# Scale and shift of the first norm, moved from the ends of the MLP into its middle, with the result kept in DRAM

## The chip, the cores and the metric

The kernel runs on one core of a Trainium2 chip. The metric is device time of one execution in microseconds (us), lower is better. The profile comes from one further execution of the same program; its times are counted from the start of the span.

## The reference

Two layers process 512 latent tokens and, in the first layer only, 256 context tokens, each of width 1024. Only the end of a layer matters here:

```python
x_mid = layer_norm(ALPHA * x + gt1 * mix, ln1_g[l], ln1_b[l])
ff = squared_relu_mlp(x_mid * (1.0 + sc2) + sh2, mlp_w1[l], mlp_w2[l])
x = layer_norm(ALPHA * x_mid + gt2 * ff, ln2_g[l], ln2_b[l])
```

A layer norm subtracts a row's mean, divides by its deviation, and then multiplies by `g` and adds `b`, both vectors of 1024 channels. `x_mid` is used twice: as the MLP's input (the channel mixing) and as the residual of the second norm.

## The kernel before

Tokens are handled in tiles of 128 rows by 1024 channels: six in layer 0 (latent tiles 2 to 5, context tiles 0 and 1), four in layer 1. A layer ends in four steps: the output projection (`out_proj`, PSUM tiles `po`), the first norm tile by tile (`norm_tile` in `done`), the transposition of the normalized tiles into the MLP's input (`to_T`, PSUM tiles `pT`, results `xh` and `xl`), the MLP (`mlp`), and the second norm (`done2`). The MLP walks over eight slices `f` of the hidden channels; each does a first product (PSUM tiles `ph`) and a second one (PSUM tiles `pf`, added to `ff` on VectorE, L1814). Weights come through `raw` (L204, 512 KB loads on SyncE's queue into two buffers `wraw`) and `unit` (L215 on ScalarE and L216 on VectorE split them into a high and a low part `whi` and `wlo`). PSUM tiles of the products rotate through four banks.

The normalized tile is stored to DRAM (`xm`) without `g` and `b` of the first norm. For the MLP's input these are folded into the scale and shift of `to_T`. For the second norm's residual, `residual` loads a tile of `xm` into one of three buffers `lnx` and applies the two rows `gr2` on GpSimd (POOL), one multiplication (L1691) and one addition (L1692) over 128x1024. In the text `fetch2` calls it three times before the last slice's second product and then once after each finished tile; but a scheduler orders the instructions of each engine by a simulated timeline, and it places loads as soon as their buffers are free.

`norm_tile` is the second place that matters: L1700 adds the residual and sums the row, L1702 on ScalarE sums the squares, L1703 to L1713 are eleven VectorE instructions on one number per row (Newton steps L1711 and L1712 on `lst` and `lsi`), and L1714 on ScalarE writes the normalized tile.

Of the kernel before, what the change touches and what calls it, by code (L numbers as in the profile page):

```python
# [8 lines left out]
F32 = mybir.dt.float32  # L9
# [18 lines left out]
D = 1024  # L28
T = 768
# [105 lines left out]
class Net:  # L135
# [62 lines left out]
    def raw(self, src, stage=None):  # L198

        if stage is None:  # L200
            r = self.wp.tile([128, 1024], F32, name="wraw", bufs=2)
        else:
            r = stage.tile([128, 1024], F32, name="wraw", bufs=12)
        self.nc.sync.dma_start(r, src)  # L204
        return r

    def unit(self, src, stage=None):
# [667 lines left out]
    def qkv(self, l, hi, lo, A, ctx_out, tick, gate):  # L875
# [25 lines left out]
        def norm(raw, t0, x):  # L901

            g, cg, sg = tab[x]
            n = (6 - t0) * 4
            r = raw[:, t0:].rearrange("p t h d -> p (t h) d")
            ss = p.tile([128, 24], F32, name="nss", bufs=2)
            for t in range(t0, 6):
                w = p.tile([128, 4, 64], F32, name="nsq")
                nc.scalar.activation(w, raw[:, t], AF.Square)
                v.reduce_sum(ss[:, 4 * (t - t0):4 * (t - t0) + 4], w, axis=AX.X)  # L910
            v.tensor_scalar(ss[:, :n], ss[:, :n], 1.0 / 64, RMS_EPS, op0=ALU.mult, op1=ALU.add)
            rs = self.rsqrt(p, ss[:, :n], n, "nr", 24)
            v.tensor_mul(r, r, rs.unsqueeze(2).to_broadcast([128, n, 64]))
            if t0 == 0:
                c = raw[:, 0:2].rearrange("p t h d -> p (t h) d")
                nc.gpsimd.tensor_tensor(c, c, g.unsqueeze(1).to_broadcast([128, 8, 64]), op=ALU.mult)
            for t in range(4):
                o = p.tile([128, 4, 64], F32, name="nro")
                def hv(a):
                    return a.rearrange("p x (a h d) -> p x a h d", a=2, h=2)  # L920
                v.tensor_mul(hv(o), hv(raw[:, t + 2])[:, :, :, ::-1],
                             sg[:, t].rearrange("p (a h d) -> p a h d", a=2, h=2)
                             .unsqueeze(1).to_broadcast([128, 4, 2, 2, 16]))
                nc.gpsimd.tensor_tensor(raw[:, t + 2], raw[:, t + 2], cg[:, t].unsqueeze(1).to_broadcast([128, 4, 64]),
                                        op=ALU.mult)
                v.tensor_add(raw[:, t + 2], raw[:, t + 2], o)
# [32 lines left out]
        def keys(raw):  # L959
            norm(raw, 0, 1)  # L960
            for h in range(4):
                if h in GK:
                    gblock()
                ks = p.tile([128, 6, 2, 64], F32R, name="qs", bufs=2)
                nc.scalar.copy(ks[:, :, 0], raw[:, :, h])
                v.tensor_sub(ks[:, :, 1], raw[:, :, h], ks[:, :, 0])
                kf = ks.bitcast(F32)
                kT = p.tile([128, T], F32R, name="kT", tag="qT", bufs=2)
                T_((kf, 0), 0, (kT[:64], kT[64:]), 64)
                nc.sync.dma_start(A["k"][h].bitcast(F32), kT.bitcast(F32))  # L970
                kT = p.tile([128, T], F32R, name="kT", tag="qT", bufs=2)
                T_((kf, 0), 1, (kT[:64],), 64)
                tick(1.3)
                for x in range(2):
                    nc.sync.dma_start(A["kl"][h, 64 * x:64 * x + 64].bitcast(F32), kT[:64].bitcast(F32))
# [740 lines left out]
    def affine(self, l, ln, lm, sc, sh):  # L1716

        v = self.nc.vector
        m = self.modv[lm]
        g = self.cp.tile([128, 2, 8], F32, name=f"ag{l}{ln}")  # L1720
        b = self.cp.tile([128, 2, 8], F32, name=f"ab{l}{ln}")
        s1 = m[:, :, 8 * sc:8 * sc + 8]
        v.tensor_mul(g, s1, self.v(l, f"ln{ln}_g").unsqueeze(1).to_broadcast([128, 2, 8]))
        v.tensor_mul(b, s1, self.v(l, f"ln{ln}_b").unsqueeze(1).to_broadcast([128, 2, 8]))
        v.tensor_add(b, b, m[:, :, 8 * sh:8 * sh + 8])
        return g, b
# [43 lines left out]
            if t >= 2:  # L1770
                done(t)

    def mlp(self, l, hi, lo, ctx, tt, ff, p, pm, late, fetch, done):


        nc, v = self.nc, self.nc.vector
        spans = [(TC, TL)] + ([(0, TC)] if ctx else [])
        for f in range(8):
            hh = pm.tile([128, 4, T], F32R, name="hh", tag="q4", bufs=4)
            hl = pm.tile([128, 4, T], F32R, name="hl", tag="q4", bufs=4)  # L1780
            if f:
                parts = [(b, spans) for b in range(4)]
            else:
                parts = [(b, [s]) for s in spans for b in range(4)]
            U1 = {}
            for b, sp in parts:
                if b // 2 not in U1:
                    U1[b // 2] = self.unit(self.i["mlp_w1"][l, 0, 2 * f + b // 2])
                    if l + 1 < L and b == 0:
                        self.mod_unit(l + 1, f)  # L1790
                wh, wl = U1[b // 2]
                if f == 0 and b == 0 and sp[0][0] == 0:
                    late()
                for o, n in sp:
                    ps = self.pd.tile([128, 512], F32, name="ph", tag="pd")
                    self.mmB(ps[:, :n], wh, wl, 128 * (b % 2), hi, lo, o, n, 8, 256)
                    r = p.tile([128, 512], F32, name="hr", bufs=2)
                    nc.scalar.activation(r[:, :n], ps[:, :n], AF.Relu)
                    q = p.tile([128, 512], F32, name="hq", bufs=2)
                    v.scalar_tensor_tensor(q[:, :n], ps[:, :n], 0.0, r[:, :n], op0=ALU.max, op1=ALU.mult)  # L1800
                    nc.scalar.activation(hh[:, b, o:o + n], q[:, :n], AF.Copy)
                    v.tensor_sub(hl[:, b, o:o + n], q[:, :n], hh[:, b, o:o + n])

            if l + 1 < L and f == 7:
                self.mod_end(l + 1, 0, 16)

            def job(c, t):
                ps = self.pd.tile([128, 512], F32, name="pf", tag="pd")
                self.mmA(ps, *U[c], hh, hl, 128 * t, 4, 512)
                d = ff[t][:, 512 * c:512 * c + 512]  # L1810
                if f == 0:
                    nc.scalar.copy(d, ps)
                else:
                    v.tensor_add(d, d, ps)  # L1814
            if M1 + f - 1 == 24:
                self.mod_end(l, 2 * M1, 48)
            U = []
            if f < 7:
                for c in range(2):
                    U.append(self.unit(self.i["mlp_w2"][l, f, c]))  # L1820
                    if c == 0 and f and M1 + f - 1 < 24:
                        self.mod_unit(l, M1 + f - 1)
                    for t in tt:
                        job(c, t)
            else:
                for _ in range(3):
                    fetch()
                for c in range(2):
                    U.append(self.unit(self.i["mlp_w2"][l, f, c]))
                for t in tt:  # L1830
                    job(0, t)
                    job(1, t)
                    if t >= 2:
                        done(t)


    def forward(self):
        nc, v = self.nc, self.nc.vector
# [10 lines left out]
        hi, lo = self.split_pair(px)  # L1849
# [4 lines left out]
        for u in range(8):  # L1854
            self.mod_unit(0, u, p0, cols)
            if u >= 2:
                t = (LAT + CTX)[u - 2]
# [13 lines left out]
        for l in range(L):  # L1871
            ctx = l < L - 1
            tt = LAT + (CTX if ctx else [])
# [75 lines left out]
            pm = self.pool(f"pm_{l}", es=eh)  # L1949
# [3 lines left out]
            ph = self.pool(f"ph_{l}", es=eh)  # L1953
# [4 lines left out]
            xm = self.dp.tile([T, D], F32, name=f"xm{l}")  # L1958
# [23 lines left out]
            hi, lo = self.split_pair(px)  # L1982
# [6 lines left out]
            ff = {t: fa[:, t] for t in tt}  # L1989
            gr2 = [self.row(ph, self.i[f"ln1_{x}"][l], "ln" + x) for x in "gb"]  # L1990
            if not ctx:
                gr3 = [fa[:, 0], fa[:, 1]]
                for g, x in zip(gr3, "gb"):
                    nc.sync.dma_start(g, self.i[f"ln2_{x}"][l].partition_broadcast(128))
            res2, later2 = {}, list(tt)

            def fetch2():
                t = later2.pop(0)
                res2[t] = self.residual(ph, xm[128 * t:128 * t + 128], gr2)
            xn = self.dp.tile([T, D], F32, name=f"xn{l}")  # L2000

            def done2(t):
# [11 lines left out]
            def late():  # L2014
                self.to_T(hi, lo, ph, "hq", y6, *ag, 1)

            self.mlp(l, hi, lo, ctx, tt, ff, ph, pm, late, fetch2, done2)
            if ctx:
                hi, lo = self.split_pair(px)
                ag = self.affine(l, 2, l + 1, 1, 0)  # L2020
# [29 lines left out]
```

## Time and profile before

| | |
|---|---|
| median of 3 runs | 3540.79 us (3539.16 to 3541.75) |
| the profiled execution | 3549.5 us, its span 3547.4 us |
| TensorE (PE) busy | 3214.4 us, 91% of the span |
| VectorE (DVE) busy | 2222.9 us, 63% |
| ScalarE (ACT) busy | 1556.0 us, 44% |
| GpSimd (POOL) busy | 458.4 us, 13% |
| granted TensorE clock, mean | 0.941 |

The busy shares are means over stages with different limits. The profiled execution is 8.7 us longer than the median of the three runs; 2.1 us of its time lie outside its span.

### The profile page before, as it was taken

How to read it: one execution, taken by the hardware profiler on the slowest of the kernel's cores; microseconds unless marked ns; L12 is line 12 of the kernel's file. 1: busy time of each engine (PE TensorE's matmuls, PEld its weight loads, DVE VectorE, ACT ScalarE, POOL GpSimd, SP SyncE). 2: the span in 40 equal slices, each digit the busy share in tenths (PEclk: the TensorE clock that was granted, in tenths of full speed). 3: DMA queues.
4: the chain of work that ended last, by engine and by line, in shares of the span. 5: the costliest groups of instructions: out<-in, count | busy, mean ns of one | idle time of the engine just before them, and what ended most of it. 6: DMA issues, size and time to landing. Idle time of an engine off the chain costs nothing. (4 is left out here: it accounts for less than half of the span.)

```text
span 3547.4 us, 62497 instructions
## 1 busy us (share of the span) xinstructions
PE 3214.4 (91%) x24309; PEld 2663.3 (75%) x24309; DVE 2222.9 (63%) x4528; ACT 1556.0 (44%) x3146; POOL 458.4 (13%) x615
## 2 busy tenths in 40 slices
PE   7999999979997997999999798878969997979996
PEld 5888888857765897888888686766857775867775
DVE  2888378856878346333335697748948786563445
ACT  2444456556776213322222353436657673233222
POOL 0102022222000121000001001212224000420000
PEclk9999999978998998999999899989969998989998
DMA  5545566575542543222322445437656526533331
GB/s 185 159 136 158 170 181 193 172 194 137 147 127 74 168 144 119 81 93 90 108 72 74 133 136 161 147 104 216 194 170 152 133 70 192 178 123 119 113 107 66
DMA packets 419535, 487.32 MB, mean 137 GB/s; under 512 B 235940, under 2 KB 302500, under 8 KB 419112
## 3 DMA queue, kind: packets, MB, share of 16 engines
q1 hardware_dynamic: 408744, 458.02, 42.3%
q0 software_dynamic: 10496, 25.31, 2.7%
q8 instruction: 192, 3.15, 0.4%
q14 instruction: 103, 0.84, 0.1%
HBM read 355.27 MB, written 127.94 MB: 136 GB/s over the span
## 5 line engine op out<-in xcount | busy, mean ns | idle before, releaser
L215 ACT CAST whi<-wraw 128x1024 fp32r<-128x1024 f32 x288 | 293.4, 1048 | 555.6 <-PE pf L322 162.0
L216 DVE TENSOR_TENSOR wlo<-wraw,whi 128x1024 fp32r<-128x1024 f32 x288 | 360.1, 1272 | 243.2 <-ACT whi L215 240.1
L310 PE MATMUL ph<-xh,whi 128*128 128x512 f32 (+1 forms) x768 | 277.1, 362 | 2.4 <-DVE xTf L1744 2.4
L311 PE MATMUL ph<-xl,whi 128*128 128x512 f32 (+1 forms) x768 | 276.0, 360 | 3.0 <-DVE xl L1746 3.0
L312 PE MATMUL ph<-xh,wlo 128*128 128x512 f32 (+1 forms) x768 | 276.0, 360 | 0.0
L320 PE MATMUL pf<-whi,hh 128*128 128x512 f32 x640 | 253.4, 396 | 1.1 <-DVE ff L1814 0.6
L321 PE MATMUL pf<-wlo,hh 128*128 128x512 f32 x640 | 252.6, 395 | 0.0
L322 PE MATMUL pf<-whi,hl 128*128 128x512 f32 x640 | 251.6, 397 | 0.0
L1066 DVE TENSOR_REDUCE st<-pS 128x1 f32<-128x384 f32 x288 | 152.1, 536 | 116.3 <-PE pS L1064 113.8
L310 PE MATMUL pga<-xh,whi 128*128 128x512 f32 (+1 forms) x576 | 213.3, 370 | 1.6 <-ACT kT L950 1.6
L311 PE MATMUL pga<-xl,whi 128*128 128x512 f32 (+1 forms) x576 | 211.3, 367 | 0.0
L312 PE MATMUL pga<-xh,wlo 128*128 128x512 f32 (+1 forms) x576 | 210.5, 365 | 0.0
L1814 DVE TENSOR_TENSOR ff<-ff,pf 128x512 f32<-128x512 f32 x140 | 94.9, 686 | 177.9 <-PE pf L322 177.8
L1067 ACT ACTIVATE P<-pS,st 128x384 f32<-128x384 f32 x288 | 164.1, 572 | 77.0 <-DVE st L1066 72.3
L1691 POOL TENSOR_TENSOR lnx<-lnx,lng 128x1024 f32<-128x1024 f32 x14 | 35.8, 2565 | 1039.1 <-DMA lnx<-xm 1005.6
L310 PEld LDWEIGHTS ph<-xh,whi 128*128 128x128 f32 x768 | 146.1, 190 | 30.5 <-issue 2.9
L311 PEld LDWEIGHTS ph<-xl,whi 128*128 128x128 f32 x768 | 146.0, 190 | 27.2 <-DVE xl L1746 3.5
L310 PE MATMUL pm<-yh,whi 128*128 128x512 f32 (+1 forms) x384 | 141.5, 373 | 25.6 <-ACT whi L215 19.7
L312 PEld LDWEIGHTS ph<-xh,wlo 128*128 128x128 f32 x768 | 145.7, 190 | 23.5
L1101 DVE TENSOR_TENSOR pl<-pPT,ph 128x512 fp32r<-128x512 f32 x208 | 141.4, 684 | 32.9 <-ACT ph L1100 31.4
L320 PE MATMUL pat<-whi,xh 128*128 128x256 f32 x512 | 148.6, 290 | 2.0 <-ACT kT L950 1.8
L1063 PE MATMUL pS<-kT,qT 128*128 128x384 f32 x288 | 127.6, 444 | 23.0 <-ACT P L1067 18.1
(468 smaller groups left out, 8706.7 us busy)
## 6 DMA issues: line engine op xcount, KB each, us to landing
wraw<-in_mlp_w_dram SPq DMA_DIRECT2D x128, 512.0 KB
wraw<-in_w_in_dram SPq DMA_DIRECT2D x108, 512.0 KB
wraw<-in_mod_w_dram SPq DMA_DIRECT2D x96, 512.0 KB
SUV<-rV SPq DMA_DIRECT2D x192, 64.0 KB
BK<-rBK SPq DMA_DIRECT2D x24, 512.0 KB
rZK<-ZK SPq DMA_DIRECT2D x20, 512.0 KB
Z<-rZK SPq DMA_DIRECT2D x40, 256.0 KB
G<-gst SPq DMA_DIRECT2D x24, 384.0 KB
```

The lines of the kernel that those rows point to most:

```text
L215: nc.scalar.copy(h[:, c], r)
L216: nc.vector.tensor_sub(lo[:, c], r, h[:, c])
L310: nc.tensor.matmul(ps, h, a, start=(first and k == 0), stop=False)
L311: nc.tensor.matmul(ps, h, b, start=False, stop=False)
L312: nc.tensor.matmul(ps, lw, a, start=False, stop=(last and k == kt - 1))
L320: nc.tensor.matmul(ps, a, h, start=(k == 0), stop=False)
L321: nc.tensor.matmul(ps, a, lw, start=False, stop=False)
L322: nc.tensor.matmul(ps, b, h, start=False, stop=(k == kt - 1))
L1063: nc.tensor.matmul(ps[:, :w], qT[h][:, o:o + 128], kT[:, ks], start=True, stop=False)
L1066: v.reduce_max(nm, ps[:, :w], axis=AX.X, negate=True)
L1067: nc.scalar.activation(P[:, ks], ps[:, :w], AF.Exp, bias=nm, accum_out=sm)
L1101: v.tensor_sub(pl, pt, ph)
```

## The change

`residual` with `gr2` is called inside the MLP, once after each weight unit of the second product from the second slice on (`affine`): it loads a tile of `xm`, multiplies and adds on GpSimd, and GpSimd's own queue stores the result to a new DRAM tensor `xr`. The second norm's residual is then loaded from `xr`, with nothing to apply. Both kinds of load are ordered behind the last weight load that was issued before them (`issue_after`), so that the scheduler can't place them earlier.

```diff
         else:
             r = stage.tile([128, 1024], F32, name="wraw", bufs=12)
-        self.nc.sync.dma_start(r, src)
+        self.w_dma = self.nc.sync.dma_start(r, src)
         return r
...
                     if c == 0 and f and M1 + f - 1 < 24:
                         self.mod_unit(l, M1 + f - 1)
+                    if f:
+                        affine()
                     for t in tt:
                         job(c, t)
...
-            res2, later2 = {}, list(tt)
+            xr = self.dp.tile([T, D], F32, name=f"xr{l}")
+            res2, later2, plain = {}, list(tt), list(tt)
+
+            def affine():
+
+                if plain:
+                    t = plain.pop(0)
+                    rows = slice(128 * t, 128 * t + 128)
+                    with self.tc.issue_after(self.w_dma.ins):
+                        x = self.residual(ph, xm[rows], gr2)
+                    nc.gpsimd.dma_start(xr[rows], x)
 
             def fetch2():
                 t = later2.pop(0)
-                res2[t] = self.residual(ph, xm[128 * t:128 * t + 128], gr2)
+                with self.tc.issue_after(self.w_dma.ins):
+                    res2[t] = self.residual(ph, xr[128 * t:128 * t + 128], None)
```

TensorE's order of instructions is the same in both programs. On SyncE's queue, between the output projection and the MLP of layer 0, three loads of `xm` stand between the stores of the normalized tiles before:

```order
L1689 DMA lnx<-in_x_dram 128x1024
L1689 DMA lnx<-xm_15002 128x1024
L1977 DMA xm_15002<-y_14998 128x1024 x2
L1689 DMA lnx<-xm_15002 128x1024
L204 DMA wraw<-in_mod_w_dram 128x1024 x2
L1689 DMA lnx<-xm_15002 128x1024
L1977 DMA xm_15002<-y_14998 128x1024 x2
L204 DMA wraw<-in_mlp_w_dram 128x1024 x2
L260 DMA modp_93<-modo 2x256 x4
```

Now none is there; the first two stand in the MLP's second slice, one behind each unit:

```order
L1689 DMA lnx<-in_x_dram 128x1024
L1979 DMA xm_15002<-y_14998 128x1024 x2
L204 DMA wraw<-in_mod_w_dram 128x1024 x2
L1979 DMA xm_15002<-y_14998 128x1024 x2
L204 DMA wraw<-in_mlp_w_dram 128x1024 x2
L260 DMA modp_93<-modo 2x256 x4
L204 DMA wraw<-in_mlp_w_dram 128x1024 x6
L204 DMA wraw<-in_mod_w_dram 128x1024 x2
L204 DMA wraw<-in_mlp_w_dram 128x1024 x2
L260 DMA modp_93<-modo 2x256 x4
L204 DMA wraw<-in_mlp_w_dram 128x1024 x2
L204 DMA wraw<-in_mod_w_dram 128x1024 x2
```

```order
L1689 DMA lnx<-xm_15002 128x1024
L204 DMA wraw<-in_mlp_w_dram 128x1024 x2
L1689 DMA lnx<-xm_15002 128x1024
L260 DMA modp_90<-modo 2x256 x4
```

Moved: three of six loads left the stretch between norm and MLP; the other three left the stretch behind the MLP, where loads of `xr` took their place.

On VectorE, in the transposition of layer 1, the order before was (`xTf` and `xl` make the transposed input, `lst` and `lsi` are the norm's numbers, `wlo` the low part of a weight unit):

```order
L1744 TENSOR_SCALAR xTf<-pT,ag_32904,ab_32905 128x256
L1701 TENSOR_SCALAR lst<-lst 128x1
L1711 SCALAR_TENSOR_TENSOR lst<-lsi,lst 128x1
L1744 TENSOR_SCALAR xTf<-pT,ag_32904,ab_32905 128x256
L1712 SCALAR_TENSOR_TENSOR lsi<-lst,lsi 128x1
L1744 TENSOR_SCALAR xTf<-pT,ag_32904,ab_32905 128x256
L1746 TENSOR_TENSOR xl<-xTf,xh 128x2x256
L1713 TENSOR_TENSOR lst<-lst,lsi 128x1
L1746 TENSOR_TENSOR xl<-xTf,xh 128x2x256
L1703 TENSOR_SCALAR lst<-lst 128x1
```

and is now:

```order
L1744 TENSOR_SCALAR xTf<-pT,ag_32923,ab_32924 128x256
L1701 TENSOR_SCALAR lst<-lst 128x1
L1711 SCALAR_TENSOR_TENSOR lst<-lsi,lst 128x1
L1712 SCALAR_TENSOR_TENSOR lsi<-lst,lsi 128x1
L216 TENSOR_TENSOR wlo<-wraw,whi 128x1024
L1713 TENSOR_TENSOR lst<-lst,lsi 128x1
L1744 TENSOR_SCALAR xTf<-pT,ag_32923,ab_32924 128x256 x2
L1746 TENSOR_TENSOR xl<-xTf,xh 128x2x256
L1703 TENSOR_SCALAR lst<-lst 128x1
L1746 TENSOR_TENSOR xl<-xTf,xh 128x2x256
```

Moved: half of a weight unit's split (L216) now stands ahead of L1713 and of the first pair of `xl`.

On GpSimd, at the end of layer 1, four pairs of multiplication and addition now each end in a store:

```order
L1691 TENSOR_TENSOR lnx<-lnx,lng 128x1024
L1692 TENSOR_TENSOR lnx<-lnx,lnb 128x1024
L2007 DMA xr_33023<-lnx 128x1024
L1691 TENSOR_TENSOR lnx<-lnx,lng 128x1024
L1692 TENSOR_TENSOR lnx<-lnx,lnb 128x1024
L2007 DMA xr_33023<-lnx 128x1024
```

No pair is left behind the last matmuls.

## Rows read from the trace of the kernel before

**Rows 1.** Busy time by engine in four stretches: A, B, C and D.

```profile
1366.00:1391.00 25.00, 7.65 (x50) 6.23 (x52) 22.19 (x45) 14.21 (x23) 12.24 (x5) 0.60 0.44 147
1948.00:1982.00 34.00, 14.15 (x58) 9.98 (x58) 32.88 (x88) 20.10 (x30) 5.48 (x9) 0.65 0.42 139
3123.00:3153.00 30.00, 6.61 (x30) 4.46 (x28) 26.38 (x48) 14.70 (x24) 12.69 (x6) 0.66 0.55 189
3507.00:3544.00 37.00, 12.56 (x53) 9.50 (x51) 33.26 (x76) 9.55 (x12) 5.38 (x2) 0.70 0.14 51
```

**Rows 2.** PE's waits, 1920 to 2010: us, times, longest.

```profile
PE pT L1737 <- DVE ff L1814: 8.9, 3, 5.9
```

**Rows 3.** Timeline of POOL, stretch B: start, us, instruction.

```profile
1937.37 2.40 POOL L1691 TENSOR_TENSOR lnx<-lnx,lng 128x1024 f32<-128x1024 f32 x1 [551.97 <-DMA lnx<-xm]
1939.84 3.39 POOL L1692 TENSOR_TENSOR lnx<-lnx,lnb 128x1024 f32<-128x1024 f32 x1
```

**Rows 4.** Timeline of DVE at the same place.

```profile
1937.59 2.19 DVE L1711 SCALAR_TENSOR_TENSOR lst<-lsi,lst 128x1 f32<-128x1 f32 x1
...
1940.90 2.36 DVE L1712 SCALAR_TENSOR_TENSOR lsi<-lst,lsi 128x1 f32<-128x1 f32 x1
```

**Rows 5.** DVE by line, 1340 to 1362, POOL idle: count, busy us, mean ns.

```profile
L1711 DVE SCALAR_TENSOR_TENSOR lst<-lsi,lst 128x1 f32<-128x1 f32 x12 | 2.6, 217 | 0.3
L1712 DVE SCALAR_TENSOR_TENSOR lsi<-lst,lsi 128x1 f32<-128x1 f32 x12 | 1.9, 157 | 0.2
L1713 DVE TENSOR_TENSOR lst<-lst,lsi 128x1 f32<-128x1 f32 x3 | 0.5, 154 | 0.0
```

**Rows 6.** DVE by line, 1930 to 1985.

```profile
L1711 DVE SCALAR_TENSOR_TENSOR lst<-lsi,lst 128x1 f32<-128x1 f32 x17 | 13.9, 820 | 0.1
...
L1712 DVE SCALAR_TENSOR_TENSOR lsi<-lst,lsi 128x1 f32<-128x1 f32 x17 | 4.8, 285 | 0.1
L1746 DVE TENSOR_TENSOR xl<-xTf,xh 128x512 fp32r<-128x512 f32 x6 | 4.0, 690 | 0.0
```

**Rows 7.** Timeline of DVE: three of the last slice's additions in layer 0.

```profile
1934.19 0.69 DVE L1814 TENSOR_TENSOR ff<-ff,pf 128x512 f32<-128x512 f32 x1 [0.46 <-PE pf L322]
...
1936.99 0.69 DVE L1814 TENSOR_TENSOR ff<-ff,pf 128x512 f32<-128x512 f32 x1 [0.21 <-PE pf L322]
...
1965.54 0.68 DVE L1814 TENSOR_TENSOR ff<-ff,pf 128x512 f32<-128x512 f32 x1
```

**Rows 8.** DVE by line, 1362 to 1392.

```profile
L1711 DVE SCALAR_TENSOR_TENSOR lst<-lsi,lst 128x1 f32<-128x1 f32 x6 | 7.0, 1160 | 0.1
...
L1713 DVE TENSOR_TENSOR lst<-lst,lsi 128x1 f32<-128x1 f32 x3 | 2.6, 881 | 0.0
L1712 DVE SCALAR_TENSOR_TENSOR lsi<-lst,lsi 128x1 f32<-128x1 f32 x6 | 2.6, 438 | 0.1
```

**Rows 9.** Timeline of DVE, ahead of stretch A.

```profile
1363.10 2.35 DVE L1713 TENSOR_TENSOR lst<-lst,lsi 128x1 f32<-128x1 f32 x1
```

**Rows 10.** DVE by line, 3125 to 3157.

```profile
L1746 DVE TENSOR_TENSOR xl<-xTf,xh 128x512 fp32r<-128x512 f32 x7 | 9.8, 1412 | 0.1
L1712 DVE SCALAR_TENSOR_TENSOR lsi<-lst,lsi 128x1 f32<-128x1 f32 x5 | 4.2, 848 | 0.1
L1711 DVE SCALAR_TENSOR_TENSOR lst<-lsi,lst 128x1 f32<-128x1 f32 x5 | 2.7, 545 | 0.0
```

**Rows 11.** Timelines of PE and of DVE, end of stretch C.

```profile
3152.61 0.50 PE L311 MATMUL ph<-xl,whi 128*128 128x512 f32 x1 [2.29 <-DVE xl L1746]
...
3153.39 1.95 DVE L1746 TENSOR_TENSOR xl<-xTf,xh 128x512 fp32r<-128x512 f32 x1
```

**Rows 12.** DVE by line, 3507 to 3548.

```profile
L1711 DVE SCALAR_TENSOR_TENSOR lst<-lsi,lst 128x1 f32<-128x1 f32 x12 | 4.6, 395 | 0.1
L1712 DVE SCALAR_TENSOR_TENSOR lsi<-lst,lsi 128x1 f32<-128x1 f32 x12 | 3.9, 334 | 0.1
```

**Rows 13.** Busy time in one slice of the MLP of layer 0.

```profile
1503.00:1579.00 76.00, 76.00 (x408) 61.81 (x407) 28.46 (x41) 19.12 (x31) 0.00 (x0) 1.00 0.30 98
```

More of the change, by code (lines that the diff above doesn't have):

```diff
@@ L1771, in out_proj, with mlp @@
                 done(t)
-    def mlp(self, l, hi, lo, ctx, tt, ff, p, pm, late, fetch, done):
+    def mlp(self, l, hi, lo, ctx, tt, ff, p, pm, late, affine, fetch, done):
         nc, v = self.nc, self.nc.vector
@@ L2015, in late @@
                 self.to_T(hi, lo, ph, "hq", y6, *ag, 1)
-            self.mlp(l, hi, lo, ctx, tt, ff, ph, pm, late, fetch2, done2)
+            self.mlp(l, hi, lo, ctx, tt, ff, ph, pm, late, affine, fetch2, done2)
             if ctx:
```

## The prediction

> **What bounds the kernel now.** TensorE (PE) is busy for 91% of the span, so I looked first for the stretches where it is not, in the view of busy time by stretch. Around the change there are four [rows 1]; a row gives the stretch, its length, the busy time of PE, its weight loads, VectorE (DVE), ScalarE and GpSimd (POOL), then the granted PE clock. A is the norm and transposition of layer 0, B the end of its MLP, C the norm and transposition of layer 1, D the end of the kernel. PE works 7.65 of 25 us in A, 14.15 of 34 in B, 6.61 of 30 in C, 12.56 of 37 in D. DVE works 22.19, 32.88, 26.38 and 33.26 us there, 88 to 97%. PE's waits in B name DVE first [rows 2]. So in these stretches DVE is the bound, and whatever shortens its work there shortens the kernel.
>
> The second view is the timeline of POOL and of DVE side by side. In B POOL starts a multiplication over a 128x1024 tile at 1937.37, for 2.40 us [rows 3]. At 1937.59 DVE starts L1711, which works on one number per row, and needs 2.19 us for it; the next Newton step, beside POOL's second operation, needs 2.36 [rows 4]. While POOL is idle the same lines need 0.217 and 0.157 us [rows 5]. So DVE does not compute there, it stands until POOL's operation ends, once per operation. Of POOL's 20 such operations on this residual (10 tiles, two each) all lie in or just ahead of these four stretches.
>
> **The change part by part.**
>
> *The operations leave the four stretches.* For each I take the busy time of the small DVE lines and subtract their count times the undisturbed mean [rows 5].
>
> B: L1711 13.9 - 17 x 0.217 = 10.2; L1712 4.8 - 17 x 0.157 = 2.1; together 12.3 us [rows 6]. Not all comes back. The additions of the last slice's products come 2.80 us apart at 1934.19 and 1936.99, at PE's pace; six more follow, so the last is due at 1936.99 + 6 x 2.80 = 1953.8 at the earliest. It ran at 1965.54 [rows 7]: 11.7 us. DVE will wait a little between them, so I take 11.0, with 9 and 12.3 as the ends. The residual's load is no new wait: POOL had its tile by 1937.37 [rows 3], and the same load now serves DVE directly.
>
> A: L1711 5.7, L1712 1.7, L1713 2.1, together 9.5 us [rows 8]. The 2.35 us of L1713 at 1363.10 [rows 9] lie ahead of A, while PE still makes the last output projections, so I count half of its 2.1: 8.5, ends 7.4 and 9.5.
>
> C: the Newton steps lose 3.4 and 1.6. L1746 has two inputs of 128x512; it takes 0.690 undisturbed [rows 6], here 9.8 for seven, so it loses 5.0; together 10.0 us [rows 10]. Two deductions. PE resumes the MLP at 3152.61, and the last stretched L1746, 1.95 long, starts behind that [rows 11]: 1.3 us were hidden. And half of a weight unit's split now stands ahead of L1713 (the order in the section on the change); it needs a load that is only issued when the unit before it is split, and I estimate 1.6 us of waiting for it. That leaves 7.1; ends 5 and 10.
>
> D: L1711 4.6 - 12 x 0.217 = 2.0, L1712 3.9 - 12 x 0.157 = 2.0; 4.0 us [rows 12]. DVE is the bound to the last instruction, so all of it counts.
>
> *They arrive in the MLP.* Ten pairs, each 4.8 us of POOL by its shorter operations [rows 3], one behind each weight unit of the second product. There PE is busy 76.00 of 76.00 us and DVE 28.46 [rows 13]. PE fills one of four PSUM banks per 2.80 us [rows 7], so it runs three pieces, 8.4 us, ahead of a DVE that stands; a pair takes 4.8. I take 0. If the cover were gone: 10 x 4.8 = 48 us.
>
> *Ten stores from POOL and ten loads more.* 10.5 MB in all. In a slice at most 2.1 MB are added to 76 us x 98 GB/s = 7.4 MB, at a DMA share of 0.30 [rows 13]: it rises to about 0.39. What waits for a store is a load in the MLP's last slice. POOL has nothing else queued there. SyncE's queue gets one load behind a pair of weight loads and ahead of the next pair, which waits for its buffer anyway. I take 0; 3 us if the three loads of `xr` ahead of the last slice's weights delay something.
>
> *Three loads leave SyncE's queue between norm and MLP.* They stood ahead of weight loads, so the weights can only come earlier; PE's waits in B name DVE, not weights [rows 2], so I take 0, with a gain left to the last rival.
>
> *The clock.* In A, B and C the granted clock is 0.60 to 0.66 [rows 1], a mix of the two levels 1.2 and 2.4 GHz, since PE works little. With 8 to 11 us less of waiting PE still waits over 10 us in each, so I expect the same falls: 0. At most, with a full clock throughout, 28.4 us of PE work in A, B and C by some 0.36 would give 10.
>
> Sum: 8.5 + 11.0 + 7.1 + 4.0 = 30.6 us. Against the profiled execution 3549.5 gives 3518.9; that execution is 8.7 us above the median of the runs shown, so the median becomes 3540.8 - 30.6 = 3510.2. The ends of the terms give 25.4 to 35.8 less 3 for the loads: 3505 to 3518.
>
> **The rivals.**
>
> *Half comes back.* When DVE no longer stands, the chain of norm and transposition (DVE to ScalarE to DVE to ScalarE to PE) ends last in A and C. For it: DVE is busy 88 to 89% there, not 97% as in B [rows 1], so other waits exist already. Against it: that chain itself runs through the stretched lines. With B and D alone, 11.0 + 4.0 = 15.0: 3525.8.
>
> *Slower: the stalls move and are exposed.* Each pair in the MLP holds up DVE where PE waits for it at once: at the seam from first to second product, where the last `hl` (L1802) is needed within a few us, or where a weight unit's `wlo` is late. If every pair cost its 4.8 us, 48 - 30.6 = 17 us slower, 3558; it decides from 30.6 / 10 = 3.1 us per pair on. Against it: the loads stand behind units of the second product, away from that seam, and DVE works 37% of the time [rows 13]. The Trainium skill, in SBUF — State Buffer, section Who interferes with whom, says that a DVE instruction with two SBUF inputs and a GpSimd instruction that reads SBUF take turns, and the second blocks until the first is finished; the 2.19 us beside a POOL operation of 2.40 agree [rows 3, 4]. By that rule the standing is not removed, only moved, which speaks for this rival. The same section says that a DVE instruction with at most one SBUF input does not contend; by that, L1814, whose other input is in PSUM, would run on beside POOL and only splits and `hl` would stand, which no row here shows.
>
> *No change.* The long rows hide something else that DVE waits for, which stays. Against it: they begin with a POOL operation and end with it in all four stretches. 3541.
>
> *More than the sum.* All 35.8 us come back and the clock doesn't fall: up to 46 us, 3495.
>
> **How the numbers follow.** The forecast has 0.62, half 0.20, more than the sum 0.08, no change 0.05, slower 0.05. A measurement can tell about 0.2% (7 us) from no change. The first three are all faster: 0.90; same 0.05; slower 0.05. The range for 8 in 10 takes in the forecast's own 3505 to 3518, the better part of half a gain (down to 14 us) and the lower part of more: 3500 to 3527.
>
> **What would show it.** In the profile after: no POOL operation of L1691 or L1692 between the last `po` and the first `ph` except those of layer 1's first norm, and none behind the last `pf`; L1711 and L1712 at 0.22 and 0.16 us in A, B and D; B some 11 us shorter, A 8 to 9, C 7, D 4. In the MLP some `wlo` or `hl` rows of 2 to 3 us more, and PE without waits there. Wrong would be: PE waiting for L1802 or L216 inside the MLP; or the four stretches as long as before with DVE idle in them, waiting for ScalarE.

## The result and the profile after

The changed kernel took 3504.01 us (median of four runs, 3496.50 to 3509.48) beside 3539.97 us for the kernel before: a ratio of 0.9902, 95% interval 0.9877 to 0.9926, by which it takes 34.7 us less (26 to 44). Run once more as a control, it gave 0.9914 (0.9896 to 0.9931). Forecast were 30.6 us less, 3510.2, with 3500 to 3527.

The two profiled executions differ by more, 53.0 us of span (3547.4 and 3494.4). So I compared them by place: for an instruction that is in both traces, its start after less its start before. The difference grows or shrinks only where one of the two loses time. A ScalarE instruction of the first product (L1798) at the start of the MLP of layer 0 starts at 1431.87 before and 1411.57 after (-20.30), one near its end at 1900.15 and 1879.85 (-20.30 again): nothing happened between. The table gives what each stretch contributed, each kernel's profiled execution against that of before, in us. The stretches are taken a little wider here than in [rows 1], so that what is still open at their ends is in them; on the time of before, A runs from 1340 to 1431, B from 1900 to 2011, C from 3107 to 3200, D from 3501 to the end. "Layer 0 ahead of A" and "layer 1 ahead of C" hold no edited instruction.

| stretch | forecast | changed kernel | control |
|---|---|---|---|
| layer 0 ahead of A | 0 | -10.8 | -3.9 |
| A | -8.5 | -9.5 | -9.5 |
| MLP of layer 0 | 0 | 0.0 | 0.0 |
| B | -11.0 | -11.2 | -11.2 |
| layer 1 ahead of C | 0 | -7.4 | -3.9 |
| C | -7.1 | -9.6 | -6.9 |
| MLP of layer 1 | 0 | 0.0 | 0.0 |
| D | -4.0 | -4.5 | -4.5 |

A to D give 34.8 us in the one execution and 32.1 in the other, the ratios of the runs 34.7 and 30.4. The 18.2 us ahead of A and C (7.8 in the control) are scatter of the attention stages from one execution to the next: layer 0 ahead of A, where no kernel is edited, lies between -12.4 and +2.2 us over thirteen profiled executions, and the one of before that all are compared with is itself 8.7 us above the median of the first three runs of its kernel.

The pairs of GpSimd are now in the MLP. Its timeline in the changed kernel, second slice of layer 0 (start, us, instruction):

```profile
1476.24 2.39 POOL L1691 TENSOR_TENSOR lnx<-lnx,lng 128x1024 f32<-128x1024 f32 x1 [186.34 <-DMA lnx<-xm]
1478.71 2.40 POOL L1692 TENSOR_TENSOR lnx<-lnx,lnb 128x1024 f32<-128x1024 f32 x1
1481.40 0.58 POOL L2007 DMA_DIRECT2D xr<-lnx  x1 [0.30 <-POOL lnx L1692]
1490.12 3.16 POOL L1691 TENSOR_TENSOR lnx<-lnx,lng 128x1024 f32<-128x1024 f32 x1 [8.13 <-DMA lnx<-xm]
```

Nothing like it stands in B any more. The small lines of the norm there (1905 to 1953), grouped (count, busy us, mean ns), answer to [rows 6]:

```profile
L1746 DVE TENSOR_TENSOR xl<-xTf,xh 128x512 fp32r<-128x512 f32 x6 | 3.9, 683 | 0.0
L1711 DVE SCALAR_TENSOR_TENSOR lst<-lsi,lst 128x1 f32<-128x1 f32 x17 | 3.6, 214 | 0.1
L1712 DVE SCALAR_TENSOR_TENSOR lsi<-lst,lsi 128x1 f32<-128x1 f32 x16 | 2.5, 154 | 0.1
```

The 17 L1711 take 3.6 us where they took 13.9. The last addition of the MLP of layer 0, due at 1953.8 by TensorE's pace and run at 1965.54 [rows 7], is now at TensorE's pace but for 0.75 us (3.55 us behind the one ahead of it, in place of 2.80). VectorE's timeline:

```profile
1927.89 0.69 DVE L1814 TENSOR_TENSOR ff<-ff,pf 128x512 f32<-128x512 f32 x1 [0.40 <-PE pf L322]
...
1930.69 0.69 DVE L1814 TENSOR_TENSOR ff<-ff,pf 128x512 f32<-128x512 f32 x1 [0.21 <-PE pf L322]
...
1934.24 0.68 DVE L1814 TENSOR_TENSOR ff<-ff,pf 128x512 f32<-128x512 f32 x1
```

In the MLP itself TensorE is busy throughout, as in [rows 13], with 11.49 us of GpSimd in the same slice and a DMA share of 0.40 in place of 0.30:

```profile
1483.00:1559.00 76.00, 76.00 (x407) 61.91 (x400) 27.88 (x39) 18.73 (x30) 11.49 (x6) 1.00 0.40 133
```

VectorE hardly stands in the MLPs. In the two of them two of its instructions take 0.3 us or more over what is usual for them, both `hl` in layer 1, 2.50 and 2.69 us in place of 0.69; in other places it is GpSimd that waits, as at 1490.12. The first of the two:

```profile
3175.36 2.50 DVE L1802 TENSOR_TENSOR hl<-hq,hh 128x512 fp32r<-128x512 f32 x1 [0.70 <-ACT hh L1801]
```

Why the same program gives -9.6 us in C once and -6.9 another time is a matter of the clock. Up to the last transposed piece the two agree: that ScalarE instruction starts at 3153.50 before, 3106.48 after and 3117.17 in the control, 8.1 and 7.7 us earlier against the start of C. The rest lies in the first 13 us of the MLP's products, where the granted clock (last but two) differs. Before, the changed kernel, and the control:

```profile
3152.00:3156.00 4.00, 3.39 (x9) 2.68 (x10) 3.89 (x6) 0.56 (x1) 2.70 (x2) 0.62 0.84 253
3156.00:3160.00 4.00, 4.00 (x18) 3.22 (x17) 2.27 (x4) 0.56 (x1) 0.00 (x0) 0.95 0.04 13
```

```profile
3105.00:3109.00 4.00, 3.77 (x16) 2.82 (x17) 3.86 (x8) 1.74 (x4) 0.00 (x0) 1.00 0.83 227
3109.00:3113.00 4.00, 4.00 (x19) 3.22 (x18) 1.03 (x2) 0.00 (x0) 0.00 (x0) 1.00 0.11 41
```

```profile
3116.00:3120.00 4.00, 4.00 (x10) 2.95 (x10) 3.86 (x8) 1.42 (x3) 0.00 (x0) 0.50 0.78 260
3120.00:3124.00 4.00, 4.00 (x16) 3.22 (x15) 0.71 (x2) 0.00 (x0) 0.00 (x0) 0.83 0.02 6
```

TensorE was back at 2.4 GHz with the first product in the one execution, and still at 1.2 GHz for some 5 us in the other.

### The profile page after: what moved, and what is told of

Read it like the earlier page. It is cut to its first block, busy times and chain, and to the rows that moved or that the text cites. A ratio compares the mean times of both kernels' runs of the same rounds, so it can differ in the third digit from the quotient of the medians.

```text
span 3494.4 us, 62529 instructions
## 1 busy us (share of the span) xinstructions
PE 3196.2 (91%) x24309; PEld 2649.9 (76%) x24309; DVE 2190.2 (63%) x4528; ACT 1555.9 (45%) x3146; POOL 462.7 (13%) x625
## 5 line engine op out<-in xcount | busy, mean ns | idle before, releaser
L216 DVE TENSOR_TENSOR wlo<-wraw,whi 128x1024 fp32r<-128x1024 f32 x288 | 358.7, 1266 | 242.8 <-ACT whi L215 232.8
L1814 DVE TENSOR_TENSOR ff<-ff,pf 128x512 f32<-128x512 f32 x140 | 94.8, 685 | 177.5 <-PE pf L322 177.3
L310 PEld LDWEIGHTS ph<-xh,whi 128*128 128x128 f32 x768 | 145.0, 189 | 30.4 <-issue 2.9
L321 PE MATMUL pat<-wlo,xh 128*128 128x256 f32 x512 | 147.0, 287 | 0.0
```

Of the source, the lines that this page charges most:

```text
L216: nc.vector.tensor_sub(lo[:, c], r, h[:, c])
L310: nc.tensor.matmul(ps, h, a, start=(first and k == 0), stop=False)
L321: nc.tensor.matmul(ps, a, lw, start=False, stop=False)
```

## The experiments

My theory: a GpSimd operation on the residual makes VectorE stand, and A to D are bound by VectorE, so what counts is whether a pair lies in these stretches. Rivals: the copy in DRAM or the places of the loads made the gain by themselves; the pairs' cost in the MLP is not zero but small by luck. Gains are worked out from the ratio and the median of the kernel before that ran beside it. This table holds the contributions by stretch of all profiled executions, read as the one above.

| kernel | ratio (95%) | gain, us | A | B | layer 1 ahead of C | C | D |
|---|---|---|---|---|---|---|---|
| control | 0.9914 (0.9896-0.9931) | 30 | -9.5 | -11.2 | -3.9 | -6.9 | -4.5 |
| order alone | 0.9949 (0.9932-0.9966) | 18 | -8.2 | +0.1 | -4.3 | -8.3 | 0.0 |
| no scale and shift | 0.9907 (0.9893-0.9921) | 33 | -8.5 | -10.7 | -3.5 | -10.1 | -4.3 |
| no order | 0.9959 (0.9942-0.9975) | 15 | +4.1 | -10.7 | -6.9 | -2.3 | -4.5 |
| on VectorE | 0.9973 (0.9957-0.9990) | 10 | -6.2 | -3.2 | -3.5 | +2.6 | -2.0 |
| three pairs per tile | 0.9907 (0.9887-0.9928) | 33 | -9.3 | -11.1 | -0.3 | -9.5 | -4.4 |
| one input, before | 0.9932 (0.9916-0.9949) | 24 | -3.4 | -3.6 | -21.9 | -2.4 | -1.3 |
| one input, after | 0.9854 (0.9834-0.9873) | 52 | -8.7 | -10.6 | -24.5 | -9.2 | -3.5 |
| fourth tile | 0.9904 (0.9890-0.9919) | 34 | -9.5 | -11.5 | -5.3 | -11.3 | -4.1 |
| fourth tile, one input | 0.9849 (0.9826-0.9871) | 53 | -9.6 | -10.8 | -24.0 | -13.4 | -3.1 |
| one input, layer 1 | 0.9918 (0.9902-0.9933) | 29 | -9.0 | -11.1 | +0.1 | -9.3 | -3.6 |
| one input, layer 0 | 0.9866 (0.9849-0.9883) | 47 | -9.6 | -10.8 | -27.8 | -7.0 | -4.5 |

**The control.** The changed kernel, unaltered.

> The changed kernel once more, as a control beside the other kernels. Theory (VectorE stood while GpSimd scaled and shifted the residual; the change took those operations out of the four stretches where VectorE is the bound): 34.6 us less than before, the sum of 9.5 + 11.2 + 9.5 + 4.3 read from the two traces in A, B, C and D. Rival (part of the 34.7 us measured is drift between executions, as the 18 us by which the two profiled executions differ elsewhere): anything from 25 to 45 us.

30 us, 24 to 37: the theory's 34.6 is inside, and the sum of its four stretches, 32.1, nearer still.

**The order alone.**

```diff
-                res2[t] = self.residual(ph, xm[128 * t:128 * t + 128], gr2)
+                with self.tc.issue_after(self.w_dma.ins):
+                    res2[t] = self.residual(ph, xm[128 * t:128 * t + 128], gr2)
```

> The kernel before with the second half of the change alone: the loads of the second norm's residual are ordered behind the last weight load, there is no copy in DRAM, and GpSimd still scales and shifts all ten tiles. In layer 0 three pairs now come in the MLP's last slice and three behind it, in layer 1 three and one. Theory: the stretches A and C lose their pairs and B and D keep theirs, so 9.5 + 9.5 = 19 us less than before (15 to 22). Rival, the copy in DRAM is what helps: no difference. Rival, a pair in the last slice is exposed: less than 15.

18 us (12 to 24), from A and C, with B and D as before. Half the change is only this: loads that the scheduler had pulled forward are held back into the last slice. The three pairs there ran under TensorE's work: the MLP's length was unchanged.

**No scale and shift.** Without the two GpSimd instructions the residual lacks the first norm's `g` and `b`.

```diff
-                res2[t] = self.residual(ph, xm[128 * t:128 * t + 128], gr2)
+                res2[t] = self.residual(ph, xm[128 * t:128 * t + 128], None)
```

> The kernel before without the scale and shift of the first norm in the second norm's residual: both GpSimd instructions of each of the ten tiles are left out, so that the residual lacks g and b. The loads stay where they were. Theory: everything that the change gained comes from GpSimd's operations standing in VectorE's way, so this gains as much, 30 to 38 us. Rival, the places of the loads on SyncE's queue made the gain: no difference to before.

33 us (28 to 38), by the same four stretches, with every load where it stood before. The change loses nothing against leaving the work out, and gains nothing by the places of its loads.

**No order.** The changed kernel without its two `issue_after` (two lines, the reverse of the edit above).

> The changed kernel without the order behind the weight loads: the copy in DRAM stays, the loads go as early as their buffers are free. By the program's order all six pairs of layer 0 then come between the output projection and the start of the MLP, and all four of layer 1 likewise. Theory: B and D are free of pairs, 11.2 + 4.3 = 15.5 us less than before, but A has six pairs in place of three and C four in place of three, which gives back up to 9.5 + 3.2: 3 to 15 us less than before. Rival, the order is ornament: 34.6 less.

15 us (9 to 21): B and D come back, A gets worse. In one point the expectation failed: C, with four pairs in place of three, was to be up to 3.2 us longer than before and is 2.3 us shorter, and why stays open. GpSimd's timeline of this kernel shows A with six pairs; three of the twelve operations:

```profile
1366.62 2.66 POOL L1691 TENSOR_TENSOR lnx<-lnx,lng 128x1024 f32<-128x1024 f32 x1 [3.55 <-DMA lnx<-xm]
1369.36 2.35 POOL L1692 TENSOR_TENSOR lnx<-lnx,lnb 128x1024 f32<-128x1024 f32 x1
...
1398.52 3.18 POOL L1691 TENSOR_TENSOR lnx<-lnx,lng 128x1024 f32<-128x1024 f32 x1 [2.52 <-DMA lnx<-xm]
```

So the copy in DRAM without the order would have been about half the change, as the order without the copy; the runs don't tell the two halves apart (9 to 21 and 12 to 24).

**On VectorE.** The kernel before with `nc.vector` for the two instructions.

```diff
-            nc.gpsimd.tensor_tensor(xt, xt, rows[0], op=ALU.mult)
-            nc.gpsimd.tensor_tensor(xt, xt, rows[1], op=ALU.add)
+            eng.tensor_tensor(xt, xt, rows[0], op=ALU.mult)
+            eng.tensor_tensor(xt, xt, rows[1], op=ALU.add)
...
+                res2[t] = self.residual(ph, xm[128 * t:128 * t + 128], gr2, nc.vector)
```

> The kernel before with the residual's scale and shift on VectorE itself, in the old places: 20 instructions of 128x1024. Theory: VectorE no longer stands (34.6 us) and does 20 x 1.14 = 22.8 us of work more, most of it where it is the bound: about 12 us less than before (5 to 20). Rival, the operations stood on another limit than VectorE: 0 to 23 us more.

10 us (4 to 15). A helper engine that makes the bound engine stand 2.2 us per operation is worse here than no helper: VectorE's own rows for the two lines are 1.22 us each (busy us, mean ns):

```profile
L1692 DVE TENSOR_TENSOR lnx<-lnx,lng 128x1024 f32<-128x1024 f32 x10 | 12.2, 1222 | 8.9 <-DMA lnx<-xm 8.9
L1693 DVE TENSOR_TENSOR lnx<-lnx,lnb 128x1024 f32<-128x1024 f32 x10 | 12.2, 1217 | 0.0
```

**Three pairs per tile.** The changed kernel with two more pairs on each tile, which makes the residual another one.

```diff
                         x = self.residual(ph, xm[rows], gr2)
+                    for _ in range(2):
+                        nc.gpsimd.tensor_tensor(x, x, gr2[0], op=ALU.mult)
+                        nc.gpsimd.tensor_tensor(x, x, gr2[1], op=ALU.add)
                     nc.gpsimd.dma_start(xr[rows], x)
```

> The changed kernel with two more pairs of multiplication and addition per tile on GpSimd in the MLP, so that the residual is not the right one: 14.4 us of GpSimd per tile in place of 4.8. Theory (VectorE only stands one GpSimd operation of 2.4 us at a time and then has its turn, with 8.4 us of PSUM banks ahead of it): as the changed kernel, within 5 us. Rival (VectorE stands through the whole of it): 14.4 - 8.4 = 6 us per tile come out, 60 us more than the changed kernel. Rival (every pair costs its time somewhere): 96 us more.

33 us (26 to 40), as the changed kernel, and at most 0.3 us in the two MLPs together. The stalls are there, and hidden: in this slice GpSimd works 39.53 of 76 us and VectorE 39.83, 12 us more than in the changed kernel, and TensorE doesn't wait. Over both MLPs 31 of VectorE's instructions take at least 0.3 us more than is usual for them, 53 us in all.

```profile
1483.00:1559.00 76.00, 76.00 (x396) 62.23 (x395) 39.83 (x40) 19.53 (x30) 39.53 (x17) 1.00 0.40 132
```

VectorE's timeline beside a GpSimd that works through seven operations from 1474.54 to 1493.23, less than 0.1 us apart:

```profile
1480.73 1.85 DVE L1802 TENSOR_TENSOR hl<-hq,hh 128x512 fp32r<-128x512 f32 x1 [0.70 <-ACT hh L1801]
...
1485.46 0.69 DVE L1814 TENSOR_TENSOR ff<-ff,pf 128x512 f32<-128x512 f32 x1 [0.35 <-PE pf L322]
1487.92 6.40 DVE L216 TENSOR_TENSOR wlo<-wraw,whi 128x1024 fp32r<-128x1024 f32 x2 [1.77 <-ACT whi L215]
```

`hl` and the two `wlo` stand (1.85 and 6.40 us; 0.69 and 2.36 where GpSimd is idle), L1814, with one input in PSUM, does not (0.69). That is the other half of the rule of the Trainium skill that the prediction left open (SBUF — State Buffer, section Who interferes with whom: a VectorE instruction with at most one SBUF input, outside its two-port modes, does not contend), and the trace agrees.

**One input.** By that rule the stalls could be avoided without moving anything. The kernel before with the norm's small lines in another form:

```diff
-            v.scalar_tensor_tensor(a, rs, xm, rs, op0=ALU.mult, op1=ALU.mult)
-            v.scalar_tensor_tensor(rs, a, 1.5, rs, op0=ALU.add, op1=ALU.mult)
-        v.tensor_mul(nb, nmu, rs)
+            v.tensor_scalar(a, rs, xm, rs, op0=ALU.mult, op1=ALU.mult)
+            v.tensor_scalar(rs, a, 1.5, rs, op0=ALU.add, op1=ALU.mult)
+        v.tensor_scalar(nb, nmu, rs, None, op0=ALU.mult)
```

> The kernel before with the three small lines of the norm (the two Newton steps and the product that follows) written as tensor-scalar instructions, with one tensor in SBUF as input and the other numbers as per-partition scalars; all of the residual's work stays on GpSimd where it was. Theory (a VectorE instruction with two tensor inputs from SBUF takes turns with GpSimd, one with a single input does not): these lines fall from 2.2 to 0.2 us beside GpSimd, and of 9.5 + 11.2 + 5.0 + 4.3 = 30 us as much comes back as the large two-input instructions behind them don't lose in their place: 10 to 30 us less than before. Rival (every VectorE instruction on SBUF stands, or scalars that come from SBUF count as inputs): no difference.

24 us, inside the range, but partly by luck: only 10.7 us come from A to D, which the expectation was about, and 21.9 from layer 1 ahead of C (more on that below). The form does what the rule says. All 60 L1711 of this kernel, 19 of them beside one of GpSimd's operations on the residual, by minimum, median and maximum in ns:

```profile
L1711 DVE TENSOR_SCALAR lst<-lsi,lst x60: 260/269/276, 1348.2 to 3507.5; 128x1 f32<-128x1 f32 x60
```

But the next large instruction with two inputs stands in their place, here in B:

```profile
1942.98 2.20 DVE L1700 SCALAR_TENSOR_TENSOR ff<-lnx,ff 128x1024 f32<-128x1024 f32 x1
1945.11 0.08 DVE L1700 DVE_READ_ACCUMULATOR ff<-lnx,ff 128x1 f32 x1
1945.11 3.42 DVE L2003 TENSOR_TENSOR ff<-ff,gtr 128x1024 f32<-128x1024 f32 x1
```

GpSimd's operation from 1944.17 took 3.27 us: it waited for L1700, and L2003 for it. Moving the pairs away is worth three times as much in these stretches (32.1 to 34.8 us) as making the small lines immune.

**One input, after.** The same form in the changed kernel.

> The changed kernel with the three small lines of the norm as tensor-scalar instructions. Left in its norms is one pair of GpSimd, that of the fourth tile of layer 1's first norm, beside which two Newton steps took 2.30 and 2.42 us in place of 0.16 and 0.22. Theory: they fall to 0.2 and C gets 3 to 4.3 us shorter: 38 us less than before. Rival: the large instructions behind them stand instead, as the changed kernel, 34.6.

52 us, not 38: the expectation failed. A to D give 32.0, no more than the change alone. The rest lies in layer 1 ahead of C, -24.5 where the control has -3.9. The instructions there are not edited, but the scheduler, which works with the durations that it expects, orders layer 1 anew once layer 0's norms are written otherwise. The last four kernels follow that up.

**The fourth tile.** In the changed kernel C still holds one pair, that of the fourth tile of layer 1's first norm.

```diff
+            if l:
+                xq = self.dp.tile([128, D], F32, name="xq")
+                nc.gpsimd.dma_start(xq, self.residual(ph, x_src[128 * tt[3]:128 * tt[3] + 128], gr))
...
+                if l and t == tt[3]:
+                    res[t] = self.residual(ph, xq, None)
+                else:
+                    res[t] = self.residual(ph, x_src[128 * t:128 * t + 128], gr)
```

> The changed kernel with the same treatment for the one pair of GpSimd that is left in C: the residual of the fourth tile of layer 1's first norm is scaled and shifted ahead of the output projection, kept in DRAM and loaded again. Theory: the Newton steps that took 2.30 and 2.42 us fall to 0.16 and 0.22, C is 4.3 us shorter, and the pair costs nothing in the output projection, where TensorE has work: 4 us less than the changed kernel (2 to 5). Rival, the pair stands in the way of VectorE's evacuations in the output projection: no difference, or up to 4.8 us more.

34 us (29 to 39): the runs can't tell it from the changed kernel. C is 1.7 us shorter than in the one profiled execution of that and 4.4 than in the other, so the 2 to 5 us may be there, and stay open.

**Fourth tile and one input together.**

> The fourth tile's pair moved and the three small lines as tensor-scalar instructions together. If the 17 us that the tensor-scalar form gave beyond the changed kernel come from another order of instructions that the scheduler chose in layer 1 between its projections and its attention (the trace shows them there, not in A to D), they are here too, since that order is nearly the same: 50 us less than before, with a C 1 to 4 us shorter than in the changed kernel. If they came from the norms, they are gone with the pair: 39 less.

53 us (46 to 62), as expected from the order, and C is 4.2 us shorter than with the one input alone. 3488.24 us is the lowest median of all, though its interval doesn't tell it from that of the one input alone.

**One input in layer 1 alone, and in layer 0 alone.** In the changed kernel, the form chosen by layer.

> The changed kernel with the tensor-scalar form in the norms of layer 1 alone, which lie behind layer 1's attention, so that its order of instructions there stays that of the changed kernel. If the tensor-scalar form helps by itself, C is 2 us shorter and D as before: 2 us less than the changed kernel. If it helps because it changes the scheduler's order in layer 1's attention, those 14 to 16 us are absent: 34 to 37 less than before, not 50. Rival, the form itself saves 17 us in the norms of layer 1: 50 less.

> The changed kernel with the tensor-scalar form in the norms of layer 0 alone, where no GpSimd pair is left beside them: A and B by themselves a little longer, 0.05 us for each of the seven small instructions of six tiles, some of it hidden, 1 us. But the scheduler orders layer 1 anew, and not as with the form in both layers. Theory (order of layer 1): a difference of several us to the changed kernel, of either sign, between the end of B and the start of C. Rival (the form): no difference over 2 us.

29 us (24 to 35) and 47 us (41 to 54). With the form in layer 1 alone, TensorE, GpSimd and SyncE have the changed kernel's order throughout, and nothing is gained, the 2 us hoped for in C included. With the form in layer 0 alone, where no pair stands beside it and A and B are unchanged, layer 1 ahead of C gains 27.8. In one point the expectation was wrong: the new order of layer 1 is not a third one, but up to C the same as with the form in both layers. So it is the order that gives these 18 us: 51.7 - 32.9, the form in both layers against three pairs per tile, which ran beside it, and 47.4 - 29.0, the form in layer 0 against that in layer 1. What else may come with another order, such as other places in memory, was not told apart. Of what the other order gives, one part shows in TensorE's waits in the first 230 us of layer 1 (us, times, longest), in the control and with the form in layer 0 alone:

```profile
PE pmod L251 <- DMA wraw<-in_mod_w_dram: 11.5, 3, 4.1
PE pK L676 <- DVE ca L335: 1.6, 1, 1.6
```

```profile
PE pmod L251 <- DMA wraw<-in_mod_w_dram: 4.5, 2, 4.2
```

The first of these waits is 4.2 to 6.0 us in the four kernels with that order and 9.3 to 13.0 in the ten profiled executions without it. From the ScalarE instruction at 2011.4 (before) to the first copy of `HR` behind it (L709, 2243.7 before) lie 220.4 to 222.4 us in the four and 229.3 to 232.9 in the ten. The rest of the gain lies in the attention and was not taken apart.

## Why the prediction was right, point by point

- **VectorE stands while GpSimd works, and A to D are bound by VectorE.** Shown from two sides: without the operations 33 us come back in the same four stretches, and three times the operations cost nothing where VectorE is not the bound.
- **B, 11.0.** Measured 11.2. The forecast let the last addition come back to TensorE's pace but for a little waiting; it does but for 0.75 us.
- **A, 8.5.** Measured 9.5, the upper end. The step that failed is the half deducted for L1713 ahead of A [rows 9]: the difference grew from -10.8 to -13.0 us across it, so TensorE's work there did not hide its 2.2 us.
- **C, 7.1.** Measured 9.6 and 6.9; a term mis-sized in parts. The chain gave 8.1 and 7.7, since the wait for a weight unit, put at 1.6, was 0.82. What came on top, 1.5 more in the one execution and 0.8 less in the other, is the clock at the start of the MLP, which the forecast had at zero.
- **D, 4.0.** Measured 4.5 to the end of the span.
- **The pairs cost nothing in the MLP.** 0.0 us in both MLPs, but the reason given was hardly called upon: two standing instructions of VectorE left the PSUM banks 3.8 us to cover, not 48. That they would have covered more is shown by three pairs per tile alone: 53 us of standing, and at most 0.3 us come out. The cover is also larger than I took it for: I let VectorE stand through a whole pair of 4.8 us against 8.4 of banks, but it has a turn after each operation.
- **Stores and loads, nothing.** The DMA share rose to 0.40, 0.39 was forecast, and no wait came of it.
- **The rivals.** "Half" asked that A and C stay as long, with ScalarE's part of the chain ending last. In A TensorE's two longest waits, both for VectorE's small lines, fell from 8.1 and 6.7 us to 4.0 and 3.1. In C most of its waiting is for ScalarE's L1714, before as after, but L1714 itself waits for L1713, the last of those lines, and this waiting fell from 17.3 to 12.9 us. "Slower" needed 3.1 us per pair; at most 0.03 per tile were seen, with three pairs on each. "More" asked for a clock that holds; in C it was back earlier in one execution and later in the other.

## What to carry to other kernels

Look for a helper engine's long instructions next to very short ones on the bound engine that take ten times their usual length: the helper is then not free, and the work belongs where another engine is the bound, even at the price of a trip through DRAM. Moving it needs both halves, a place for the result and an order that keeps the scheduler from pulling the loads forward again; each alone gave about half of the gain (15 and 18 us). Where a scheduler orders the program, compare by place before crediting a change: a form that did nothing where it was written gave 18 us elsewhere.

## What the runs showed of the hardware

- An instruction on one number per row stands as long as one on 1024: 2.19 to 2.36 us in place of 0.16 to 0.22 [rows 4, 5]; L2003, on 128x1024, took 3.42 in place of 1.22 in the kernel with one input. With one tensor input and per-partition scalars it never did (60 of 60 L1711 at or below 0.276 us, 19 of them beside GpSimd), at a price of 0.05 us each.
- It goes both ways. GpSimd's 2.40 us operation took 3.16 us when it started 0.33 us behind a VectorE instruction of 1.2 us with two SBUF inputs (1490.12 in the changed kernel), and 3.39 when it started 0.07 us behind one (1939.84 before [rows 3]).
- The same program got TensorE's 2.4 GHz back at the first product of an MLP once, and some 5 us later another time, 2.3 us of the span.
